# Three modulation vectors of a diffusion layer: elementwise sums on three engines, or products on TensorE

## The chip, the cores and the metric

The kernel runs on one core of a Trainium2 chip. The core has a matrix engine (TensorE, PE in the profile, with PEld for its weight loads), three engines for elementwise work (VectorE or DVE, ScalarE or ACT, GpSimd or POOL) and a queue on SyncE (SP) that issues all of this kernel's transfers. Each engine works through its own instructions in order and waits for others through semaphores. The metric is the device time of one execution in microseconds (us); lower is better.

## The reference, cut to what matters

Two layers act on 1024 latent tokens and 256 context tokens of width 1024. Every layer is modulated by six vectors per sample, once for the latent tokens and once for the context:

```python
silu_c = jax.nn.silu(c)
silu_cc = jax.nn.silu(c_ctx)
for l in range(DEPTH):
    mod = (silu_c @ w_mod[l] + b_mod[l])[:, None, :]
    mod_c = (silu_cc @ w_mod[l] + b_mod[l])[None, None, :]
    sh_m, sc_m, gt_m, sh_f, sc_f, gt_f = jnp.split(mod, 6, axis=-1)
    ...
    h = modulate(x, g_pre_mix[l], sh_m, sc_m)          # vectors 0 and 1
    y, yc = mixer(h, hc, ...)                          # attention and pooling
    x = x + gt_m * rmsnorm(y, g_post_mix[l])           # vector 2
    h = modulate(x, g_pre_ffn[l], sh_f, sc_f)          # vectors 3 and 4
    x = x + gt_f * rmsnorm(swiglu(h, ...), g_post_ffn[l])   # vector 5
```

The weights `w_mod[l]` are 1024 x 6144 in float32, so one vector reads 1024 x 1024 numbers, 4 MB, and multiplies them by only two columns (the activations of `c` and `c_ctx`). Layer 0 has dense attention (8 heads over all 1280 keys) beside a pooling mixer, layer 1 windowed attention; both end in a gated feed-forward part.

## The kernel before, in words

Activations lie feature-major: 128 features on the partitions, tokens along the row. Precision is kept by splitting a float32 operand into a rounded part and a rest (names ending in h and l: `wh`, `wl`, `hh`, `hl`, `ph`, `pl`) and adding three products. The latent tokens go in two chunks of 512 (L0, L1), the context in one of 256 (CC).

**Order.** The program is not written in the order in which it runs. `Plan` records every operation with what it depends on, `merge` interleaves parts of the record by giving each a stretch of positions, and `layout` then places all operations on the five engines by a list scheduling with a table of costs: an engine takes, of what is ready, the operation with the lowest position. Tiles come from shared pools, 38 large buffers of 4 KB a partition (tag `Q`, names beginning with `Q_`), 19 small ones of 2 KB (tag `S`), 8 banks of PSUM (`ps`). A tile that lies more than a given number of positions ahead must leave a reserve free (`AHEAD_OF`). Loads are allowed up to 30 us of PE work ahead (`LOAD_WINDOW`); a transfer is put down as 1100 ns to its start, its bytes over 360 per ns (4 bytes an element), and 1500 ns to its landing. Everything is issued from one line, so that the profile puts L419 on every instruction; the groups are told apart by their tiles.

**The stage around the change.** Vectors 0 and 1 of layer 0 are needed first. `mod_row` computes them at the start of the kernel on PE: the two columns of `c2` are the stationary operand, a 128 x 512 piece of weights (tile `S_wm`) streams past, eight such products add up in one PSUM bank, and the two rows that result (`S_row`) are turned into columns by four small transposes. Vectors 2, 3 and 4 (`MODLATE`) come later. After the first projections, one stage merges three streams: attention of L0 and CC (`attend0`); the pooling mixer with the projections of L1 (`poolmix`, `proj0`); and `mod_vec` for vectors 2, 3 and 4, followed by `fin_post` and `fin_pre`, which combine them with gains. The merge gives attention the first nine tenths of the stretch (`SHARES[0]`) and the others all of it. Then come the output projection of L0 and CC and the residual with its norms (`rest`, `chain`), which read these vectors first.

**The elementwise form.** `mod_vec` takes a vector in two halves of 512 outputs and loads eight pieces of 128 x 512 (tag `MW`, three buffers, tile `mw`). For each of the two columns it keeps an accumulator `S_ma` of 128 x 512. Of the eight pieces, with `POOLC = 2`, four go to DVE (one multiply or multiply-add each) and four are scaled on ACT (into `S_mp`, the first into the accumulator itself) and added on POOL. At the end PE transposes the accumulator in four blocks, DVE sums along the row (`mc`) and adds the bias. `mod_vec` also computes vector 5 of layer 0 and all of layer 1, in other stages.

Of the kernel before, what the change touches and what calls it, by code (L numbers as in the profile page):

```python
# [10 lines left out]
F32 = mybir.dt.float32  # L11
F32R = mybir.dt.float32r
AF = mybir.ActivationFunctionType
ALU = mybir.AluOpType
# [4 lines left out]
P = 128  # L19
D = 1024  # L20
KT = D // P
# [30 lines left out]
POOLC = 2  # L52
# [16 lines left out]
class Plan:  # L69
# [73 lines left out]
    def add(self, eng, op, args, kw):  # L143
# [29 lines left out]
        for n in tiles:  # L173
            self.tiles[n][3] += 1
        cost, fset = self.cost(eng.name, op, args, kw, outs, ins)
        load = eng.name == "SP" and all(a.space == DRAM for a in ins)
        if eng.name == "DVE":
            port = op != "stream_shuffle" and all(a.space != PSUM for a in ins + outs)
        else:
            port = eng.name == "PL" and op != "memset"  # L180
        self.ops.append((eng, op, args, kw, deps, tiles, cost, fset, i + self.bias, load, self.phase, port))

    def cost(self, e, op, args, kw, outs, ins):
        o = outs[0] if "out" in kw or e != "ACT" else args[0]
        if op == "dma_start":
            n = 4 * self.free(o) * list(o.ap)[0][1]
            return max(56.0, n / 360.0), None
        if e == "PE":
            mv = args[2]
            n = self.free(mv)  # L190
            if op == "transpose":
                return max(54.0, n / 1.2) + 2.7, None
            return max(104.0, n / 2.4 + 13.0) if mv.dtype == F32R else max(216.0, n / 0.6) + 2.7, None
        n = max(self.free(a) for a in ins + [o]) if ins else self.free(o)
        ps = any(a.space == PSUM for a in ins)
        ptr = any(self.free(a) == 1 for a in ins) and n > 1
        if e == "ACT":
            c = (51.0 if ins[0].space == PSUM else 93.0) + n / 1.2
            c += 93.0 * (self.is_ap(kw.get("bias")) or self.is_ap(kw.get("scale"))) + 93.0 * ("accum_out" in kw)
            return c, self.SETS.get(args[2].name)  # L200
        if e == "PL":
            return {"tensor_tensor": 160 + 2.13 * n, "tensor_scalar": 175 + 3.34 * n}.get(op, 40), None
        if op == "reciprocal":
            return 69 + 6.25 * n, None
        if op in ("tensor_copy", "tensor_scalar", "memset"):
            return 69 + 61 * ptr + n * (1.0417 if ps else 0.5208), None
        if op == "tensor_tensor_reduce":
            return 129 + 1.0417 * n, None
        return 69 + 61 * (ptr and op == "scalar_tensor_tensor") + 1.0417 * n, None
# [29 lines left out]
    def layout(self):  # L239
# [58 lines left out]
        while len(order) < n:  # L298
# [38 lines left out]
            for q in set(early) - {e}:  # L337
                for _, j in avail[q]:
                    heapq.heappush(future[q], (ready[j], ops[j][8], j))
                avail[q].clear()  # L340
            eng, op, args, kw, deps, tiles, cost, fset, pr, load, _, port = ops[i]
            moved = set()
            for tl in tiles:
# [83 lines left out]
def tile_dit(  # L427
# [4 lines left out]
    plan = Plan(tc.nc)  # L432
    T, S, V, G, SP = plan.engines
# [7 lines left out]
    def nm(s):  # L441
        uid[0] += 1
        return f"{s}{uid[0]}"

    def qt_(shape, dt, s="q"):
        return sb.tile(shape, dt, tag="Q", name=nm("Q_" + s), bufs=NQ)

    def st(shape, dt, s="s"):
        return sb.tile(shape, dt, tag="S", name=nm("S_" + s), bufs=NS)

    def small(shape, dt, s="t"):
        return sb.tile(shape, dt, tag="T", name=nm(s), bufs=24)

    def pst(n=512, dt=F32):
        t = ps_p.tile([P, 512], dt, tag="ps", name=nm("ps"), bufs=8)
        return t[:, :n]
# [37 lines left out]
    ident = cst.tile([P, P], F32, name="ident")  # L494
# [6 lines left out]
    c2 = cst.tile([P, KT, 2], F32, name="c2")  # L501
    bm = cst.tile([P, 2, 6, KT], F32, name="bm")
# [4 lines left out]
    mod = cst.tile([P, 2, 6, 2, KT], F32, name="mod")  # L507
# [131 lines left out]
    def mod_row(l, v0, nv):  # L639

        for b in range(2):
            acc = [pst() for _ in range(nv)]
            for k in range(KT):
                for v in range(nv):
                    w = st([P, 512], F32, "wm")
                    o = (v0 + v) * D + b * 512
                    SP.dma_start(out=w, in_=w_mod[l, k * P:(k + 1) * P, o:o + 512])
                    T.matmul(acc[v][0:2, :], c2[:, k, :], w, start=(k == 0), stop=(k == KT - 1))
            tp = pst()
            for v in range(nv):  # L650
                row = st([P, 512], F32, "row")
                S.activation(row[0:2, :], acc[v][0:2, :], AF.Copy)
                for j in range(4):
                    i = v * 4 + j
                    T.transpose(tp[:, 2 * i:2 * i + 2], row[0:2, j * P:(j + 1) * P], ident[0:2, 0:2])
            tv = tp[:, 0:nv * 8].rearrange("p (v k c) -> p v c k", v=nv, c=2)
            for v in range(nv):
                for c in range(2):
                    V.tensor_tensor(mod[:, l, v0 + v, c, b * 4:b * 4 + 4], tv[:, v, c, :], bm[:, l, v0 + v, b * 4:b * 4 + 4], op=ALU.add)

    def mod_vec(l, v, cs, pool=0):


        for half in range(2):
            acc = [st([P, 512], F32, "ma") for _ in cs]
            for k in range(KT):
                w = sb.tile([P, 512], F32, tag="MW", name=nm("mw"), bufs=3)
                o = v * D + half * 512
                SP.dma_start(out=w, in_=w_mod[l, k * P:(k + 1) * P, o:o + 512])
                for a, c in zip(acc, cs):  # L670
                    if (k + 2 * c) % 4 < pool:
                        t = a if k == 0 else st([P, 512], F32, "mp")
                        S.activation(t, w, AF.Copy, scale=c2[:, k, c:c + 1])
                        if k:
                            G.tensor_tensor(a, a, t, op=ALU.add)
                    elif k == 0:
                        V.tensor_scalar(a, w, c2[:, k, c:c + 1], None, op0=ALU.mult)
                    else:
                        V.scalar_tensor_tensor(a, w, c2[:, k, c:c + 1], a, op0=ALU.mult, op1=ALU.add)
            for a, c in zip(acc, cs):  # L680
                tp = pst()
                for j in range(4):
                    T.transpose(tp[:, j * P:(j + 1) * P], a[:, j * P:(j + 1) * P], ident)
                col = small([P, 4], F32, "mc")
                V.reduce_sum(col, tp.rearrange("p (j i) -> p j i", j=4), axis=AX.X)
                V.tensor_tensor(mod[:, l, v, c, half * 4:half * 4 + 4], col, bm[:, l, v, half * 4:half * 4 + 4], op=ALU.add)
# [5 lines left out]
    def fin_post(l, kind, cs=(0, 1)):  # L692
        for c in cs:
            V.tensor_tensor(fin[:, l, 2 * kind + 1, c, :], mod[:, l, 3 * kind + 2, c, :], gn[:, 2 * kind + 1, l, :], op=ALU.mult)
# [511 lines left out]
    plan.bias = 0  # L1206
    a = len(plan.ops)
    mod_row(0, 0, 2)
    fin_pre(0, 0)
    b = len(plan.ops)  # L1210
# [62 lines left out]
    a = len(plan.ops)  # L1273
# [18 lines left out]
    a = len(plan.ops)  # L1292
# [5 lines left out]
    b = len(plan.ops)  # L1298
# [8 lines left out]
    h = None  # L1307
    c = len(plan.ops)
    for v in MODLATE:
        mod_vec(0, v, (0, 1), POOLC)  # L1310
    fin_post(0, 0)
    fin_pre(0, 1)
    plan.merge(a, b, c, share=SHARES[0])
# [18 lines left out]
    a = len(plan.ops)  # L1332
# [4 lines left out]
    b = len(plan.ops)  # L1337
# [8 lines left out]
    a = len(plan.ops)  # L1346
    ws = ffn_pair(0, tt, SIZES[0][0], hc)
# [3 lines left out]
    b = len(plan.ops)  # L1351
# [9 lines left out]
    a = len(plan.ops)  # L1361
# [45 lines left out]
    b = len(plan.ops)  # L1407
# [22 lines left out]
    a = len(plan.ops)  # L1430
    mix = newmix(half(L0, 1))
    attend1(L0, 1, mix, AHEADS[3])
    b = len(plan.ops)
# [9 lines left out]
    a = len(plan.ops)  # L1443
# [3 lines left out]
    b = len(plan.ops)  # L1447
# [9 lines left out]
    ws = ffn_pair(1, tt, SIZES[2][0])  # L1457
# [102 lines left out]
```

## Time and profile before

| what | value |
|---|---|
| median of 3 runs | 2748.66 us (2748.55 to 2752.36) |
| the profiled execution's own time | 2747.63 us |
| its span, first to last instruction | 2745.8 us |
| granted TensorE clock, mean | 0.983 |
| busy: PE, DVE, ACT, POOL | 96%, 73%, 50%, 12% |
| moved by DMA | 481.06 MB, 175 GB/s on the mean |
| loads of modulation weights `mw` | 160 of 256 KB, 48 of them for the three vectors (130 to 361 us) |

A group's row reads: line, engine, operation, the tile written and the tiles read, their shape, the count; then busy us and the mean ns of one; then the engine's idle time just before these instructions and what ended it. A row of stages by window gives the length first and then busy us with a count for each engine. Busy time of PE is the union of its instructions' times, whose ends overlap the next one's start; two PE instructions that follow each other are therefore spaced closer than the duration of one.

### The profile page before, as it was taken

The numbers are of one execution on the slowest core, as the hardware profiler recorded it, in microseconds if no ns is written. First come the engines' busy times: TensorE is split into PE (matmuls) and PEld (weight loads), VectorE is DVE, ScalarE is ACT, GpSimd is POOL, SyncE is SP. The second block draws the span as 40 slices with busy tenths as digits, with TensorE's granted clock in tenths as the row PEclk, the third lists the DMA queues.
The fourth block names the chain that finished last, engine by engine and source line by source line (L and its number), as shares of the span: only waits on it lengthen the run. The fifth ranks groups of instructions, "written<-read, shape, count | busy, mean of one in ns | idle before, by whom it ended". The sixth has DMA issues, their size and how long they took to land.

```text
span 2745.8 us, 39261 instructions
## 1 busy us (share of the span) xinstructions
PE 2637.9 (96%) x13781; PEld 2186.7 (80%) x13781; DVE 1996.6 (73%) x3684; ACT 1361.9 (50%) x2846; POOL 319.5 (12%) x277
## 2 busy tenths in 40 slices
PE   8989898999999999999999999998999999999997
PEld 4766677888888888888878878787878788888887
DVE  4779887866559998866484688898882798872335
ACT  4468875666554333331143467677784534332011
POOL 0353532000020000000011400330000300000001
PEclk9999999999999999999999999998999999999999
DMA  7334457333566666686543635353335545556252
GB/s 285 114 102 147 141 200 276 121 110 122 177 200 216 219 215 222 226 320 223 206 151 113 219 101 190 103 176 120 116 101 203 192 173 203 196 183 253 112 184 77
DMA packets 240902, 481.06 MB, mean 175 GB/s; under 512 B 24128, under 2 KB 85824, under 8 KB 240704
## 3 DMA queue, kind: packets, MB, share of 16 engines
q1 hardware_dynamic: 240704, 478.54, 50.7%
q8 instruction: 109, 1.79, 0.3%
q14 instruction: 89, 0.73, 0.1%
HBM read 350.52 MB, written 123.99 MB: 173 GB/s over the span
## 4 chain that ended last, share of the span: by engine, by line
PE 71%; DVE 11%; ACT 4%; DMA 3%; issue 2%; POOL 1%; SPq 0%; DVEq 0%; ACTq 0%; POOLq 0%
PE ps L419 71%; DVE Q_x L419 1%; DVE S_fw L419 1%; DVE ps L419 1%; DVE mx L419 1%; ACT S_ph L419 1%; DVE Q_hl L419 1%; ACT Q_p L419 1%; DVE Q_yf L419 1%; DVE S_sq L419 1%; DMA Q_raw<-in_wo_in 1%; DVE Q_tl L419 1%; ACT S_p L419 1%; DVE S_pl L419 1%; DVE Q_wl L419 1%
## 5 line engine op out<-in xcount | busy, mean ns | idle before, releaser
L419 PE MATMUL ps<-Q_ac,Q_wh 128*128 128x512 f32 (+1 forms) x1920 | 530.3, 358 | 0.8 <-ACT Q_wh L419 0.5
L419 PEld LDWEIGHTS ps<-Q_ac,Q_wh 128*128 128x128 f32 x1920 | 343.2, 191 | 50.1 <-DVE Q_yf L419 0.6
L419 PE MATMUL ps<-Q_hh,Q_wh 128*128 128x512 f32 (+1 forms) x992 | 365.2, 377 | 6.8 <-ACT Q_hh L419 3.5
L419 PE MATMUL ps<-Q_hl,Q_wh 128*128 128x512 f32 (+1 forms) x992 | 362.6, 374 | 1.9 <-DVE Q_hl L419 1.8
L419 ACT ACTIVATE Q_wh<-Q_raw 128x1024 fp32r<-128x1024 f32 x202 | 212.4, 1063 | 303.9 <-PE ps L419 134.8
L419 PE MATMUL ps<-Q_ac,Q_wl 128*128 128x512 f32 (+1 forms) x960 | 341.7, 357 | 3.3 <-DVE Q_wl L419 3.3
L419 DVE TENSOR_TENSOR Q_wl<-Q_raw,Q_wh 128x1024 fp32r<-128x1024 f32 x190 | 235.3, 1248 | 137.7 <-ACT Q_wh L419 112.7
L419 PE MATMUL ps<-Q_tl,Q_wh 128*128 128x512 f32 x704 | 275.8, 392 | 3.1 <-DVE Q_tl L419 3.1
L419 PE MATMUL ps<-Q_th,Q_wh 128*128 128x512 f32 x704 | 275.5, 392 | 1.2 <-ACT Q_th L419 1.2
L419 PE MATMUL ps<-Q_kt,S_q 128*128 128x256 f32 (+3 forms) x992 | 255.0, 340 | 18.5 <-DVE Q_x L419 7.2
L419 PE MATMUL ps<-Q_hh,Q_wl 128*128 128x512 f32 (+1 forms) x992 | 265.9, 373 | 0.0
L419 DVE TENSOR_TENSOR S_pl<-ps,S_ph 128x512 fp32r<-128x512 f32 (+1 forms) x328 | 213.1, 672 | 69.2 <-ACT S_ph L419 64.7
L419 DVE TENSOR_TENSOR Q_yf<-Q_yf,ps 128x512 f32<-128x512 f32 (+1 forms) x200 | 116.9, 589 | 200.1 <-PE ps L419 199.7
L419 ACT ACTIVATE S_ph<-ps 128x512 fp32r<-128x512 f32 (+1 forms) x328 | 186.0, 604 | 88.3 <-PE ps L419 84.8
L419 PEld LDWEIGHTS ps<-Q_hh,Q_wh 128*128 128x128 f32 x992 | 189.8, 192 | 38.7 <-ACT Q_hh L419 5.1
L419 PEld LDWEIGHTS ps<-Q_hl,Q_wh 128*128 128x128 f32 x992 | 190.1, 192 | 30.2 <-DVE Q_hl L419 3.4
L419 PEld LDWEIGHTS ps<-Q_kt,S_q 128*128 128x128 f32 x992 | 171.0, 195 | 47.5 <-issue 12.6
L419 PEld LDWEIGHTS ps<-Q_ac,Q_wl 128*128 128x128 f32 x960 | 182.7, 190 | 28.3 <-DVE Q_wl L419 4.0
L419 PEld LDWEIGHTS ps<-Q_hh,Q_wl 128*128 128x128 f32 x992 | 175.8, 191 | 27.2
L419 PE MATMUL ps<-ident,Q_p 128*128 128x128 f32 x928 | 185.3, 277 | 10.6 <-DVE S_pl L419 3.1
L419 ACT ACTIVATE Q_p<-ps,nb 128x256 f32<-128x256 f32 (+1 forms) x336 | 185.3, 562 | 15.1 <-DVE nb L419 14.7
L419 PE MATMUL ps<-Q_th,Q_wl 128*128 128x512 f32 x704 | 188.8, 390 | 0.0
(194 smaller groups left out, 5208.9 us busy)
## 6 DMA issues: line engine op xcount, KB each, us to landing
Q_raw<-in_w_ffn_in SPq DMA_DIRECT2D x132, 512.0 KB, 4.7
a_scr_l<-S_act SPq DMA_DIRECT2D x176, 256.0 KB, 2.1
Q_ac<-a_scr_l SPq DMA_DIRECT2D x88, 512.0 KB, 6.1
mw<-in_w_mod SPq DMA_DIRECT2D x160, 256.0 KB, 3.5
Q_raw<-in_w_ffn_out SPq DMA_DIRECT2D x66, 512.0 KB, 6.8
S_q<-q_scr_l SPq DMA_DIRECT2D x192, 128.0 KB, 3.7
g_scr<-S_gs SPq DMA_DIRECT2D x88, 256.0 KB, 2.0
Q_gs<-g_scr SPq DMA_DIRECT2D x44, 512.0 KB, 5.5
```

Source lines behind the costliest of these rows:

```text
L419: getattr(eng.real, op)(*args, **kw)
```

## The change

A new function `mod_mm` takes the place of `mod_vec` for vectors 2, 3 and 4 of layer 0. It computes a half of a vector as `mod_row` does, with c2 as the stationary operand and both columns in one product. It differs from `mod_row` in its loads: a half's weights come in four transfers of 512 KB into four large buffers (`Q_wm`), and `plan.gate` makes all eight products depend on the last of the four loads. ACT copies the two rows out of PSUM, four small transposes turn them, and DVE adds the bias. `mod_vec` stays for the other vectors. `mod_mm` uses no accumulator in SBUF, no `MW` buffer and nothing on POOL.

The second edit is to the planner's table: a product with a float32 moving operand of n columns is put down as n/1.2 ns, at least 104, in place of n/0.6 ns, at least 216. That covers the products of `mod_mm`, those of `mod_row`, the sums with `ones2` in `rstd` and the sums of squares with `selg`. Prices decide only the order in which instructions are issued.

```diff
-            return max(104.0, n / 2.4 + 13.0) if mv.dtype == F32R else max(216.0, n / 0.6) + 2.7, None
+            return max(104.0, n / 2.4 + 13.0) if mv.dtype == F32R else max(104.0, n / 1.2) + 2.7, None
...
+    def mod_mm(l, v):
+
+        for b in range(2):
+            ws = []
+            for k in range(0, KT, 2):
+                w = qt_([P, 2, 512], F32, "wm")
+                o = v * D + b * 512
+                SP.dma_start(out=w, in_=w_mod[l, k * P:(k + 2) * P, o:o + 512].rearrange("(a p) n -> p a n", p=P))
+                ws += [w[:, 0, :], w[:, 1, :]]
+            plan.gate = len(plan.ops) - 1
+            acc = pst()
+            for k, w in enumerate(ws):
+                T.matmul(acc[0:2, :], c2[:, k, :], w, start=(k == 0), stop=(k == KT - 1))
+            plan.gate = None
+            row = st([P, 512], F32, "row")
+            S.activation(row[0:2, :], acc[0:2, :], AF.Copy)
+            tp = pst()
+            for j in range(4):
+                T.transpose(tp[:, 2 * j:2 * j + 2], row[0:2, j * P:(j + 1) * P], ident[0:2, 0:2])
+            tv = tp[:, 0:8].rearrange("p (k c) -> p c k", c=2)
+            for c in range(2):
+                V.tensor_tensor(mod[:, l, v, c, b * 4:b * 4 + 4], tv[:, c, :], bm[:, l, v, b * 4:b * 4 + 4], op=ALU.add)
...
     for v in MODLATE:
-        mod_vec(0, v, (0, 1), POOLC)
+        mod_mm(0, v)
     fin_post(0, 0)
     fin_pre(0, 1)
```

## The prediction

> **What bounds the kernel now.** I read the page first, then busy time by stage, then the groups of the stage that the change touches.
>
> ```profile
> span 2745.8 us, 39261 instructions
> PE 2637.9 (96%) x13781; PEld 2186.7 (80%) x13781; DVE 1996.6 (73%) x3684; ACT 1361.9 (50%) x2846; POOL 319.5 (12%) x277
> PE   8989898999999999999999999998999999999997
> ```
>
> TensorE (PE) is busy 96% of the span, so an edit that adds PE work looks bad at once. That share is a mean over unlike stages, though. The stages by window (length; then busy us and count for PE, its weight load, DVE, ACT, POOL; granted clock; DMA share; GB/s):
>
> ```profile
> 130.00:390.00 260.00, 233.56 (x1202) 174.54 (x1200) 227.00 (x409) 202.16 (x473) 116.55 (x129) 0.99 0.48 157
> 390.00:450.00 60.00, 58.95 (x318) 50.94 (x316) 42.63 (x56) 30.34 (x50) 21.80 (x16) 1.00 0.70 244
> 600.00:800.00 200.00, 199.80 (x1104) 170.29 (x1104) 108.75 (x186) 109.16 (x230) 21.77 (x12) 1.00 0.44 151
> 1600.00:2060.00 460.00, 431.54 (x2634) 368.09 (x2633) 399.43 (x1073) 348.05 (x947) 50.58 (x40) 0.96 0.40 126
> ```
>
> All the edited work lies in 130 to 390 us: attention of the first half of the latent tokens merged with the second half's projections, the pooling mixer and the three modulation vectors. There PE is not full. VectorE (DVE) is busy 227.0 of 260 (87%) and ScalarE (ACT) 202.2 (78%). In the other attention stage in which PE has gaps, 1600 to 2060, DVE stands at 399.4 of 460, again 87%; where DVE is at 54% (600 to 800) or 71% (390 to 450), PE is busy all but 0.1% and 2% of the time. So I read 87% as about what DVE reaches in this chain of hand-overs, and DVE with ACT, not PE, as the bound of this stage.
>
> PE's busy time overstates its load, since matmul ends overlap. So I count what PE needs. Its largest groups in 130 to 390:
>
> ```profile
> L419 PE MATMUL ps<-ident,Q_p 128*128 128x128 f32 x352 | 64.0, 276 | 6.3 <-DVE S_pl L419 2.8 <-ACT Q_p L419 1.9 <-DVE mc L419 0.5
> L419 PE MATMUL ps<-Q_kt,S_q 128*128 128x512 f32 x128 | 45.3, 433 | 3.9 <-ACT Q_p L419 2.9 <-DVE nb L419 0.6 <-DVE S_pl L419 0.5
> L419 PE MATMUL ps<-S_pl,Q_vt 128*128 128x512 f32 x88 | 38.2, 435 | 1.4 <-DVE S_pl L419 1.4
> L419 PE MATMUL ps<-S_ph,Q_vt 128*128 128x512 f32 x88 | 38.2, 434 | 6.4 <-ACT S_ph L419 4.9 <-DVE S_pl L419 1.4
> L419 PE MATMUL ps<-Q_hl,Q_wh 128*128 128x512 f32 x92 | 37.3, 413 | 0.0
> L419 PE MATMUL ps<-Q_hh,Q_wh 128*128 128x512 f32 x90 | 37.1, 418 | 0.4 <-ACT Q_wh L419 0.4
> L419 PE MATMUL ps<-Q_hh,Q_wl 128*128 128x512 f32 x96 | 29.9, 406 | 0.0
> L419 PE MATMUL ps<-Q_kt,S_q 128*128 128x256 f32 x96 | 20.7, 308 | 0.5 <-ACT Q_p L419 0.3
> L419 PE MATMUL ps<-ident,S_ma 128*128 128x128 f32 x48 | 9.7, 275 | 0.3 <-DVE S_fw L419 0.2
> ```
>
> What one costs when the next follows at once, from runs in the timeline (start, length, count), and from the start of the kernel, which already computes two modulation vectors by the very product that the change adds:
>
> ```profile
> 1201.41 1.07 PE L419 MATMUL ps<-Q_th,Q_wl 128*128 128x512 f32 x4
> ...
> 1202.77 0.39 PE L419 MATMUL ps<-Q_ac,Q_wl 128*128 128x512 f32 x1
> ```
> ```profile
> 372.43 1.03 PE L419 MATMUL ps<-ident,Q_p 128*128 128x128 f32 x8
> ```
> ```profile
> 23.11 0.40 PE L419 MATMUL ps<-ident,S_row 2*128 2x2 f32 x4
> ...
> 24.86 10.46 PE L419 MATMUL ps<-S_wm,c 128*2 128x512 f32 x24
> ```
> ```profile
> L419 PE MATMUL ps<-S_wm,c x64: 591/592/1062, 4.1 to 42.1; 128*2 128x512 f32 x64
> ```
>
> A split-precision product of 512 columns: (1.07 - 0.39) / 3 = 0.227 us; one of 256 columns I take at half, 0.114. A transpose: (1.03 - 0.276) / 7 = 0.108. The full-precision product of a weight half: (10.46 - 0.592) / 23 = 0.429. Need of the stage: 582 x 0.227 + 96 x 0.114 + 400 x 0.108 = 132.1 + 10.9 + 43.2; the other 124 of the 1202 instructions are small groups of mixed width, at a mean of 0.165 another 20.5. Together 206.7 us of 260: PE has 53 us to spare here.
>
> **The change, part by part.** DVE, ACT and POOL, with the rows of 130 to 390 that go:
>
> ```profile
> L419 DVE SCALAR_TENSOR_TENSOR S_ma<-mw,c,S_ma 128x512 f32<-128x512 f32 x42 | 38.1, 916 | 0.8 <-POOL S_ma L419 0.7
> ...
> L419 DVE TENSOR_REDUCE mc<-ps 128x4 f32<-128x512 f32 x10 | 6.8, 682 | 0.7 <-PE ps L419 0.6
> ...
> L419 DVE TENSOR_SCALAR S_ma<-mw,c 128x512 f32<-128x512 f32 x6 | 3.8, 640 | 0.0
> L419 DVE TENSOR_TENSOR mod<-mc,bm 128x4 f32<-128x4 f32 x10 | 3.4, 337 | 0.0
> ```
> ```profile
> L419 ACT ACTIVATE S_mp<-mw,c 128x512 f32<-128x512 f32 x42 | 29.7, 731 | 1.9 <-POOL S_ma L419 1.7
> ...
> L419 ACT ACTIVATE S_ma<-mw,c 128x512 f32<-128x512 f32 x6 | 4.4, 731 | 8.2 <-DMA mw<-in_w_mod 8.2
> ```
> ```profile
> L419 POOL TENSOR_TENSOR S_ma<-S_ma,S_mp 128x512 f32<-128x512 f32 x42 | 55.3, 1318 | 64.3 <-ACT S_mp L419 32.6 <-DVE S_ma L419 28.7 <-DVE rz L419 1.3
> ```
>
> What comes in has its rows at the start of the kernel:
>
> ```profile
> L419 ACT ACTIVATE S_row<-ps x4: 569/586/587, 22.4 to 43.1; 2x512 f32<-2x512 f32 x4
> ```
> ```profile
> L419 DVE TENSOR_TENSOR mod<-ps,bm x8: 149/152/163, 24.6 to 44.4; 128x4 f32<-128x4 f32 x8
> ```
>
> DVE loses 38.1 + 6.8 + 3.8 + 3.4 = 52.1 and gains 10 x 0.152 = 1.5: 227.0 becomes 176.4. ACT loses 29.7 + 4.4 = 34.1 and gains 6 x 0.586 = 3.5: 202.2 becomes 171.6. POOL loses 55.3 of 116.6.
>
> PE loses 48 transposes (48 x 0.108 = 5.2) and gains 48 products (48 x 0.429 = 20.6) and 24 tiny transposes (six times 0.40 = 2.4): net +17.8, to 224.5.
>
> The Trainium skill's page "FP8 and Floating Point Precision", section "TensorE Precision Notes", says that true FP32 takes four passes through the array. By that rule one product would be an estimated 4 x 0.227 = 0.91 us and the 48 together 43.6, so that PE would need 247.5. This kernel's row disagrees: 0.429 is 1.9 times 0.227, and the measurement decides.
>
> If DVE could be filled to the same 87%, the stage would need 176.4 / 0.87 = 203 us; ACT by the same share 197; PE at a complete fill 224.5. So PE becomes the bound of the stage and the length follows from how full it gets. Bounds: as full as now, 206.7 / 260 = 79.5%, gives 282 us, a loss of 22; quite full, as in 600 to 800, with 3% lost to hand-overs gives 231 us, a gain of 29. At some 242 us DVE is at 73% and ACT at 71%. The nearest row is 390 to 450 with DVE at 71%, where PE was busy 98%; ACT was lighter there (51%), and the stage still begins and ends in chains, so I take 93%: 224.5 / 0.93 = 241.4, a **gain of 18.6**.
>
> Loads. 48 loads of 256 KB become 24 of 512 KB, the same bytes, in the pool of 38 large buffers instead of three own ones. All loads go through SP's queue in program order, and these are its long waits from 130 to 450 (us, times, longest):
>
> ```profile
> SPq L419 <- DVE S_ma L419: 73.3, 26, 8.8
> SPq L419 <- POOL S_mo L419: 44.6, 11, 7.3
> SPq L419 <- ACT S_mo L419: 35.1, 9, 10.5
> ```
> ```profile
> Q_raw<-in_we_in SPq DMA_DIRECT2D x8, 512.0 KB, 5.2
> ```
>
> The first wait (a buffer that an elementwise sum still reads) goes; SP waits instead for PE to release a large buffer. The other two stay: a store waits for its producer and every load behind it waits too. The change also adds a wait: the planner sets a half's eight products behind the last of its four loads, at a landing that it puts 1.1 + 1.46 + 1.5 = 4.06 us after issue; a load of this size takes 5.2 here. If PE reaches the group just then, it stands 1.1 us, and behind it everything in its queue: scores, transposes, value products, and so DVE and ACT. Six groups, 6.8 us at most from this alone; at the least nothing, since loads may run up to 30 us of PE work ahead. I take 2, nearer to nothing because of that lead.
>
> New price in the planner. It halves the price of wide full-precision products (0.856 to 0.429), which now meets the measured 0.429. At the start this may put the 64 products' loads earlier or later among others. The bounds are PE's idle time there: it waited 6.0 us for those weights
>
> ```profile
> L419 PE MATMUL ps<-S_wm,c 128*2 128x512 f32 x64 | 32.3, 652 | 6.2 <-DMA S_wm<-in_w_mod 6.0
> ```
>
> so at best 6 us are won, and as much may be lost by the same waits doubled. I take 0. Later stages are ordered anew by the same planner; PE is full in most of them, and I take 0 there too, within the same 6 us.
>
> A result that comes late costs nothing at first: the old sums end at 396 us, and their first reader (the residual scale) starts at 444.6, which leaves 48 us of cover.
>
> ```profile
> L419 DVE TENSOR_TENSOR mod<-mc,bm x12: 86/155/1089, 203.5 to 396.5; 128x4 f32<-128x4 f32 x12
> ```
> ```profile
> 444.56 1.41 DVE L419 SCALAR_TENSOR_TENSOR Q_y<-Q_y,fin,ps 128x512 f32<-128x512 f32 x2 [0.80 <-PE ps L419]
> ```
>
> **Sum:** -18.6 + 2 + 0 = -16.6 us. The profiled execution took 2747.6 (span 2745.8 and 1.8 around it), 1.0 below the median 2748.7. So 2748.7 - 16.6 = **2732 us**. From 390 us on PE is full, so what is won before moves the rest forward without being eaten by it.
>
> **Rivals.** (A) *PE fills up.* With DVE and ACT down to three quarters, PE runs as in 600 to 800: 231 us, a gain of 29, 2748.7 - 29 = 2720. For it: the two rows with DVE at 54% and 71%. Against: this stage has many short hand-overs per product.
>
> (B) *The relief only pays the bill.* PE's gaps come from latency (transpose, split on ACT, subtraction on DVE, product), not from engine load. It then gets just the products into its gaps: 2749, no change. For it: PE's idle before its groups is a few us each, spread over many releasers. Against: 53 us of room and the same 87% twice.
>
> (C) *Late weights, slower.* A group of products reaches the head of PE's queue while its fourth load is held in SP's queue behind a store. The price is the mean wait of the row on POOL, 44.6 / 11 = 4.1 us, plus the 1.1 us of the landing: 6 x 5.2 = 31. With 31 for my 2: 2732 + 29 = 2761. It decides from 18.6 us in all, 3.1 per group; from there on nothing is left of the gain. For it: 80 us of such waits in the stage. Against: loads go ahead of need, and POOL, one cause of those waits, loses half its work.
>
> (D) *PE's additions lie on the chain and nothing is relieved:* 2748.7 + 17.8 = 2766. Against it speaks the DVE row. (E) *The four passes are real here:* 247.5 / 0.93 = 266 us of stage, 2748.7 + 6 + 2 = 2757; the x24 row all but excludes it. (F) *The change doesn't do what it says:* the planner puts the groups so late that the residual waits; over the 48 us of cover only, and then about 2749.
>
> **How the numbers follow.** My forecast 0.57 (its own range 2722 to 2743); A 0.15; B 0.12; C 0.09; D 0.04; E 0.01; F 0.02. This kernel's times can be told from no change at about 0.2%, 5.5 us: faster means below 2743.2, slower above 2754.2. Faster: 0.57 + 0.15 = 0.72, and 0.02 of B's spread: 0.74. Slower: C, D, E: 0.14. Same: 0.12. The range runs from 2714 (A with the start's 6 us) to 2753 (B with a few us of late loads): it leaves out C and D and a little besides, some 0.17.
>
> **What would show it.** The stage that now ends near 390 should end near 373, with DVE and ACT at about 73% and 71% of it and PE's count of work at 224 us; the 48 products should take 0.43 us apart and follow each other without waits for their loads; PE's idle before groups released by DVE and ACT should shrink by more than half. From there to the end, all stages should be as long as they were. I am wrong if PE's idle time in the stage stays near 26 us (B, D), if PE shows waits of over 3 us for the modulation weights (C), or if the gain or loss lies in stages after 450 us, which would be the planner's new order and not the engines' load.

## The result, and the profile after

The changed kernel takes 2788.27 us (median; 2786.43 to 2789.38) against 2748.61 us before: a ratio of 1.0144, with a 95% interval of 1.0128 to 1.0160. It is 39.7 us **slower**; the forecast was 2732 us, faster.

The page of the changed kernel begins:

```profile
span 2786.6 us, 39164 instructions
PE 2686.7 (96%) x13853; PEld 2190.0 (79%) x13853; DVE 1954.4 (70%) x3624; ACT 1341.0 (48%) x2804; POOL 258.6 (9%) x235
PE   8999999899999999999999998998999999999997
```

DVE, ACT and POOL lost 42, 21 and 61 us of busy time over the whole span (51, 31 and 55 were forecast). PE gained 48.8 us of busy time and 72 instructions, where the prediction had 48 products and 24 tiny transposes for 48 transposes: 24 instructions more. The 48 that are too many are the heart of this case. Stages of the kernel before, cut at marks that both kernels have (last store of L0's queries; last result of attention on L0; first residual scale, of L0; that of the context; that of L1; first residual scale behind a feed-forward part):

```profile
0.00:128.00 128.00, 116.62 (x533) 73.98 (x534) 74.46 (x130) 62.21 (x116) 18.68 (x19) 0.99 0.55 192
128.00:369.00 241.00, 214.69 (x1110) 162.59 (x1110) 210.77 (x379) 185.62 (x441) 113.08 (x126) 0.99 0.47 151
369.00:445.00 76.00, 74.83 (x375) 59.52 (x375) 55.85 (x80) 43.51 (x77) 23.76 (x18) 1.00 0.67 227
445.00:486.00 41.00, 31.47 (x192) 27.51 (x191) 38.60 (x66) 29.26 (x58) 5.00 (x3) 0.83 0.57 214
486.00:795.00 309.00, 307.12 (x1715) 261.21 (x1714) 188.65 (x342) 178.92 (x393) 23.72 (x16) 0.99 0.40 137
795.00:1395.00 600.00, 598.80 (x3228) 517.32 (x3227) 478.55 (x766) 204.45 (x324) 4.93 (x3) 1.00 0.66 229
1395.00:2746.00 1351.00, 1294.37 (x6639) 1084.54 (x6637) 949.68 (x1926) 657.89 (x1439) 130.35 (x93) 0.98 0.46 158
```

The same stages of the changed kernel:

```profile
0.00:136.00 136.00, 118.99 (x513) 73.86 (x514) 78.36 (x134) 63.20 (x118) 23.19 (x23) 0.95 0.52 183
136.00:393.00 257.00, 248.39 (x1189) 163.77 (x1188) 164.98 (x321) 160.13 (x397) 54.21 (x81) 1.00 0.42 132
393.00:478.00 85.00, 83.08 (x386) 59.58 (x387) 51.83 (x73) 43.62 (x77) 21.01 (x16) 1.00 0.67 230
478.00:520.00 42.00, 31.86 (x191) 27.80 (x190) 38.78 (x66) 29.36 (x58) 4.94 (x3) 0.80 0.56 205
520.00:829.00 309.00, 306.39 (x1712) 260.73 (x1711) 188.23 (x341) 179.26 (x393) 23.24 (x16) 0.99 0.40 136
829.00:1430.00 601.00, 599.46 (x3229) 517.19 (x3228) 478.17 (x766) 206.76 (x325) 4.94 (x3) 1.00 0.65 229
1430.00:2787.00 1357.00, 1298.48 (x6643) 1087.12 (x6641) 954.09 (x1926) 658.62 (x1439) 127.06 (x93) 0.97 0.46 158
```

By length: +8 before the edited stage, +16 in attention, +9 in the part that finishes it, then +1, 0, +1, and +6 in everything after 1395 us. DVE falls from 87% to 64% of the attention stage and ACT from 77% to 62%, so the relief did arrive, while PE rises from 89% to 97%: the bound has moved to PE. The view of the new weight tiles says why:

```profile
L419 PE MATMUL ps<-Q_wm,c x96: 591/592/593, 175.5 to 421.0; 128*2 128x512 f32 x96
L419 SPq DMA_DIRECT2D Q_wm<-in_w_mod x24: 367/407/985, 153.7 to 366.4; - x24
```

24 transfers bring 48 pieces of 128 x 512, and PE executes **96** instructions on them. A float32 product is two TensorE instructions. The row that the prediction quoted from the start of the kernel said so already: 64 instructions, and the loads beside it are of 32 pieces:

```profile
L419 SPq DMA_DIRECT2D S_wm<-in_w_mod x32: 327/328/925, 1.2 to 34.0; - x32
```

### The profile page after: what moved, and what is told of

The parts are those of the page before. It is cut to its first block, busy times and chain, and to the rows that moved or that the text cites. A ratio compares the mean times of both kernels' runs of the same rounds, so it can differ in the third digit from the quotient of the medians.

```text
span 2786.6 us, 39164 instructions
## 1 busy us (share of the span) xinstructions
PE 2686.7 (96%) x13853; PEld 2190.0 (79%) x13853; DVE 1954.4 (70%) x3624; ACT 1341.0 (48%) x2804; POOL 258.6 (9%) x235
## 3 DMA queue, kind: packets, MB, share of 16 engines
q1 hardware_dynamic: 240320, 478.54, 49.6%
## 4 chain that ended last, share of the span: by engine, by line
PE 69%; DVE 8%; ACT 3%; DMA 2%; issue 1%; SPq 0%; POOL 0%; DVEq 0%; ACTq 0%
PE ps L419 69%; DVE Q_x L419 1%; DVE ps L419 1%; DVE S_fw L419 1%; DVE mx L419 1%; DVE Q_tl L419 1%; DVE Q_yf L419 1%; DVE Q_hl L419 1%; ACT S_p L419 1%; DVE S_sq L419 0%; ACT Q_p L419 0%; DVE S_pl L419 0%; DVE Q_wl L419 0%; DVE S_t L419 0%; ACT S_ph L419 0%
```

## The experiments

Each variant was timed beside the kernel before on the same chip. Ratios are to that kernel, with 95% intervals.

**The new price alone.** The kernel before with the planner's second edit and nothing else:

```diff
-            return max(104.0, n / 2.4 + 13.0) if mv.dtype == F32R else max(216.0, n / 0.6) + 2.7, None
+            return max(104.0, n / 2.4 + 13.0) if mv.dtype == F32R else max(104.0, n / 1.2) + 2.7, None
```

> The kernel before with only the planner's new price (n/1.2 for a float32 product); the three vectors stay elementwise sums. Theory 1 (the products themselves are the cost: the trace after holds 96 TensorE instructions for 48 products, 0.429 us each, 41 us, and some 12 us more for changing between kinds of products 41 times): price alone costs little, 2745 to 2762, most of it the 8 us by which the stage before 136 us is already later. Theory 2 (the price misleads the planner, and its order costs the time): most of the 40 us are here, 2770 to 2790.

Measured: 2759.91 against 2748.45 us, ratio 1.0050 (1.0031 to 1.0069): 11.5 us. That is within the first theory's range and far from the second's. The price is under a third of the loss, not its body.

**The products under the old price.** The changed kernel with that line put back:

```diff
-            return max(104.0, n / 2.4 + 13.0) if mv.dtype == F32R else max(104.0, n / 1.2) + 2.7, None
+            return max(104.0, n / 2.4 + 13.0) if mv.dtype == F32R else max(216.0, n / 0.6) + 2.7, None
```

> The changed kernel with the old price (n/0.6 = 853 ns for a product of 512 columns, which is what two instructions of 0.429 us take). Theory 1: still slow by the products' PE time, 2770 to 2785, some 10 us better than the changed kernel since the plan now knows what they cost. Theory 2: 2745 or less.

Measured: 2775.85 against 2748.45, ratio 1.0112 (1.0088 to 1.0136): the products alone cost 27.4 us. With the price's 11.5 that makes 38.9 of the 39.7: the two edits add up.

**No vectors at all.** Vectors 2, 3 and 4 of layer 0 are their biases alone; their weights are neither read nor multiplied, so this time is that of a kernel with part of the computation left out. The 12 MB of loads go with the sums.

```diff
     for v in MODLATE:
-        mod_vec(0, v, (0, 1), POOLC)
+        for c_ in range(2):
+            V.tensor_scalar(mod[:, 0, v, c_, :], bm[:, 0, v, :], 1.0, None, op0=ALU.mult)
```

> The kernel before without the work on the three vectors: vectors 2, 3 and 4 of layer 0 are their biases alone, with no weights read, no sums and no products. It measures what taking the sums away is worth by itself. If VectorE and ScalarE bound the stage, as the prediction has it, the stage of 260 us shrinks to some 217 (201.5 us of PE work at 93%): 2700 to 2712. If the gaps of PE come from latency, the stage gets shorter by little more than the 5 us of removed transposes: 2735 to 2745.

Measured: 2726.22 against 2748.45, ratio 0.9924 (0.9906 to 0.9943): the elementwise sums, with their loads, cost 22.2 us. Both expectations missed: the relief is real, but half of what the prediction's reading of the bound implied. From the last store of L0's queries to the first residual scale the run without vectors shows

```profile
131.00:348.00 217.00, 203.13 (x1061) 156.69 (x1060) 165.61 (x313) 157.82 (x394) 56.92 (x84) 0.98 0.33 108
348.00:424.00 76.00, 74.37 (x374) 59.40 (x373) 51.46 (x68) 42.75 (x75) 21.76 (x16) 1.00 0.69 238
```

Attention takes 217 us in place of 241, with DVE at 76%, ACT at 73% and PE still busy only 94%: PE waits for results (its longest wait in total, from 130 to 390 us, is 6.0 us for `Q_p` of ACT) even when no other engine is near its limit. Which of the things left out, work of DVE, of ACT, of POOL or the loads, bought the 22.2 us is not told apart. Against this kernel without vectors, the products under the old price cost 2775.85 - 2726.22 = **49.6 us**, against 22.2 for the sums.

**One unbroken run for each half.** The old price, and the planner sees a half's eight products as one operation, at eight times their price and 300 ns:

```diff
-            for k, w in enumerate(ws):
-                T.matmul(acc[0:2, :], c2[:, k, :], w, start=(k == 0), stop=(k == KT - 1))
+            T.block(acc[0:2, :], c2, *ws)
...
+            if op == "block":
+                for k in range(KT):
+                    eng.real.matmul(args[0], args[1][:, k, :], args[2 + k], start=(k == 0), stop=(k == KT - 1))
+                continue
```

> The changed kernel with the old price and each half's eight products kept as one unbroken run on TensorE (6 runs in place of 41). Theory 1: the changes between kinds of products fall from 41 to 6, worth 35 x 0.30 = 10 us of PE work: some 10 us under the run with the old price, 2760 to 2775. If these changes are hidden or cost nothing, the same time as with the old price, or some us more, because a block of 6.9 us holds up attention's scores behind it.

Measured: 2772.08, ratio 1.0090 (1.0073 to 1.0107), 3.8 us under the run with the old price, with intervals that overlap: less than the 10 expected. From 130 us to the first residual scale the run with the old price, and then this one, show

```profile
130.00:472.70 342.70, 331.89 (x1560) 221.89 (x1559) 219.71 (x397) 206.95 (x476) 76.56 (x100) 1.00 0.49 159
130.00:466.90 336.90, 322.00 (x1542) 223.40 (x1541) 219.94 (x395) 204.18 (x473) 76.55 (x100) 0.99 0.49 159
```

PE's busy time fell by 9.9 us (an estimated 4 of it belong to the 18 instructions fewer, at the mean of 0.21 us), but its idle time rose from 10.8 to 14.9: part of what the unbroken runs save comes back as waiting. This run's timeline shows best what one half costs:

```profile
172.63 7.03 PE L423 MATMUL ps<-Q_wm,c 128*2 128x512 f32 x16
```

Eight products are 16 instructions and 7.03 us: (7.03 - 0.592) / 15 = 0.429 each, 0.858 for a product. Six halves are 41.2 us.

**The products twice.** The old price, with the eight products repeated (the second set starts the sum anew):

```diff
-            for k, w in enumerate(ws):
-                T.matmul(acc[0:2, :], c2[:, k, :], w, start=(k == 0), stop=(k == KT - 1))
+            for j in range(2):
+                for k, w in enumerate(ws):
+                    T.matmul(acc[0:2, :], c2[:, k, :], w, start=(k == 0), stop=(k == KT - 1))
```

> The run with the old price, but each half's eight float32 products are made twice (the second set starts the sum anew, so the result is the same): 96 more TensorE instructions, 41.2 us, nothing else. If TensorE is the bound of the stage once the sums are gone, nearly all of it shows: 2776 + 35 to 50 = 2811 to 2826. If the stage still waits mostly for other engines and the products fall into gaps of TensorE, 2780 to 2800.

Measured: 2821.04, ratio 1.0265 (1.0247 to 1.0284), 45.2 us over the run with one set. Its weight-tile view has

```profile
L419 PE MATMUL ps<-Q_wm,c x192: 590/592/593, 166.5 to 458.9; 128*2 128x512 f32 x192
```

96 instructions more cost 45.2 us, 0.47 each, and they need 0.429: once the sums are gone, all of PE's extra work shows in the time. The second set has no loads, no gate and no transposes of its own. The first set, with all of these, cost 49.6, so that by this comparison they are worth some 4 us together.

**Products in the rounded type.** The columns c2 are split into a rounded part and a rest (four stationary columns), ACT rounds the weights, and the part of the weights below the rounding is left out, which is a part of the computation. The gate goes, and the price is the old one.

```diff
+                wh = qt_([P, 2, 512], F32R, "mh")
+                S.activation(wh, w, AF.Copy)
+                ws += [wh[:, 0, :], wh[:, 1, :]]
...
-                T.matmul(acc[0:2, :], c2[:, k, :], w, start=(k == 0), stop=(k == KT - 1))
+                T.matmul(acc[0:4, :], c4[:, k, :], w, start=(k == 0), stop=(k == KT - 1))
```

> The three vectors as products in the rounded type (fp32r) in place of float32, old price: ScalarE rounds the weights, the columns are split into rounded part and rest (4 stationary columns), the rest of the weights (their part below the rounding) is left out. If the cost of the change is that a float32 product is two TensorE instructions of 0.429 us and changes the kind of product around it, then 48 instructions at 0.227 us stand here (10.9 us in place of 41) and the time falls to that of the kernel without the vectors plus about 13 us of TensorE work and up to 10 for ScalarE: 2736 to 2750. If the cost comes from the loads in large buffers, the held PSUM bank or the order of the plan, it stays at 2765 to 2780.

Measured: 2742.22 against 2749.66, ratio 0.9969 (0.9953 to 0.9984): **faster than both kernels**. Its tile view:

```profile
L419 PE MATMUL ps<-Q_mh,c x48: 387/397/479, 158.3 to 381.1; 128*4 128x512 f32 x48
...
L419 ACT ACTIVATE Q_mh<-Q_wm x24: 1041/1060/1107, 157.2 to 344.3; 128x1024 fp32r<-128x1024 f32 x24
```

The loads and their buffers are the same (24 more large tiles hold the rounded weights); now 48 instructions for 48 products, of the kind that follows at 0.227 us. The loss is gone, 33.6 us under the run with float32 products, although ACT does 25 us more. So the loads and buffers were not the cause. The gate went too in this run, but the changed kernel's view of these tiles lists no wait for their loads, and the doubled products, which add nothing to the gate, cost their full time.

**The rounding on GpSimd.** The same, with the planner's price for it added:

```diff
-                S.activation(wh, w, AF.Copy)
+                G.tensor_copy(wh, w)
```

> The rounded run (rest of the weights left out) with the 24 roundings on GpSimd in place of ScalarE. ScalarE loses 25 us of work in the stage. If the rounded run is bound by TensorE's need alone, the same time, 2738 to 2746. If ScalarE's roundings still hold up attention's splits and exponentials, up to 8 us less: 2731 to 2738. If GpSimd's slower copies make the products late, above 2746.

Measured: 2741.66 against 2747.56, ratio 0.9981 (0.9969 to 0.9993). That is the rounded run's time within the intervals: ACT's 25 us lay beside other work, as the first case has it.

**The rest of the weights too.** GpSimd subtracts the rounded weights from the weights, and eight more products a half add them, so that nothing is left out:

```diff
+                wl = qt_([P, 2, 512], F32R, "ml")
+                G.tensor_tensor(wl, w, r32(wh), op=ALU.subtract)
+                ls += [wl[:, 0, :], wl[:, 1, :]]
...
+                T.matmul(acc[0:4, :], c4[:, k, :], ls[k], start=False, stop=(k == KT - 1))
```

> As the rounded run, with the rest of the weights too: GpSimd subtracts the rounded weights from the weights, and 16 products of 0.227 us a half add up (96 instructions, 21.8 us), which is as precise as the other products of this kernel. By TensorE's work alone 11 us above the rounded run: 2747 to 2762; over that if GpSimd's 24 subtractions of some 2.6 us hold up the pooling mixer.

Measured: 2763.96 against 2749.66, ratio 1.0042 (1.0028 to 1.0056); 21.7 us over the rounded run, where 11 were expected from TensorE alone. The subtractions take 2.4 us each on POOL, beside the work of attention and the pooling mixer:

```profile
L419 POOL TENSOR_TENSOR Q_ml<-Q_wm,Q_mh 128x1024 fp32r<-128x1024 f32 x24 | 57.4, 2403 | 35.7 <-ACT Q_mh L419 21.4 <-PE ps L419 13.8 <-ACT Q_wh L419 0.4
```

From 130 us to the first residual scale PE is busy 14 us longer than in the rounded run and idle 7 us longer. It waited for the subtractions directly only 1.1 us in this profile; its longest waits are for ACT (4.7 us for `S_ph`, 4.1 for `Q_p`). That POOL makes the other 11 us is argued, not shown.

**One vector by products.** Old price; vector 4 by `mod_mm`, vectors 2 and 3 by `mod_vec`:

```diff
-        mod_mm(0, v)
+        if v == 4:
+            mod_mm(0, v)
+        else:
+            mod_vec(0, v, (0, 1), POOLC)
```

> Vector 4 by float32 products, vectors 2 and 3 by elementwise sums, old price. All three by products cost 27 us, all three left out win 22. If both sides are linear in the number of vectors, one by products costs a third, 9 us: 2755 to 2760. If the relief of VectorE and ScalarE is worth most for the first vector taken away (half of the 22 or more against 16 for the products): 2750 to 2755 or less.

Measured: 2765.69 against 2749.66, ratio 1.0047 (1.0033 to 1.0060): 16.0 us, beyond both expectations. A third of the products' 49.6 is 16.5, so taking one vector's sums away bought next to nothing here. The trace shows where. From the last store of L0's queries to the last result of attention, and from there to the first residual scale:

```profile
131.00:375.00 244.00, 217.56 (x1094) 163.67 (x1093) 202.44 (x362) 176.84 (x425) 98.71 (x113) 0.97 0.41 133
375.00:466.00 91.00, 91.00 (x403) 60.67 (x403) 52.21 (x78) 45.16 (x79) 20.24 (x16) 1.00 0.67 240
```

All 32 instructions of vector 4 start from 378.7 us on, in the part that finishes attention, where PE was full already (74.8 of 76 us before); that part is 15 us longer than before. Attention itself takes 244 us against 241, though a third of the sums is gone. Why that third buys nothing there stays open.

**Wide products' price alone.** The kernel before, with the new price only for more than two columns:

```diff
-            ... else max(216.0, n / 0.6) + 2.7, None
+            ... else max(104.0 if n > 2 else 216.0, n / 1.2) + 2.7, None
```

> The kernel before with the new price for wide float32 products alone (512 or 256 columns: the two early vectors and the sums of squares of the heads); the 2-column sums of the norms keep the old price. The new price for all cost 11 us. The wide ones take 0.858 us by the trace (two instructions of 0.429), so their new price is half the truth: if that misleads the plan, the 11 us are here, 2756 to 2762. If the narrow ones do it: 2746 to 2751.

Measured: 2755.48 against 2749.66, ratio 1.0020 (1.0008 to 1.0033): half of the price's cost, a little under the range that put all of it here. The last store of L0's queries is issued at 134.3 us, 6.0 behind the kernel before (128.3); with the whole new price it is 7.1 behind (135.4). The wide price, half the truth, goes with the late start; the rest belongs to the narrow one or to the new order as a whole.

**A price 3% lower, and 3% higher.** The kernel before with n/0.62, and in another run with n/0.58:

```diff
-            ... else max(216.0, n / 0.6) + 2.7, None
+            ... else max(216.0, n / 0.62) + 2.7, None
```

> The kernel before with the price of a float32 product 3% lower (n/0.62 in place of n/0.6), no other edit: how much the time moves when the planner only orders a little differently. If the order's own scatter is small, 2745 to 2754 and the 5 to 11 us of the runs with the new price are that price's doing. If it is 5 us and more to either side, those runs can't be told from scatter.

> As the run before it, with the price 3% higher (n/0.58). The same two outcomes: 2745 to 2754, or 5 us and more to either side.

Measured: 2748.46 and 2748.45 against 2747.56, ratios 1.0005 (0.9995 to 1.0015) and 1.0003 (0.9993 to 1.0012): no change. These small steps reorder little, though: a comparison of PE's 13781 instructions in order, line by line, with those of the kernel before gives 16 and 46 lines of difference, against 92 for the wide price and 884 for the whole one. So they show that the order doesn't scatter the time by itself at that size; they don't bound what a reordering as large as the whole price's may do.

## Why the prediction was wrong

**The step that failed: "48 products (48 x 0.429 = 20.6)".** The duration was right, the count was not. 0.429 us is the spacing of instructions, and every float32 product is two of them: 96 x 0.429 = 41.2. PE's additions were 38.4 us net in place of 17.8. The x96, the x16 in 7.03 us, the doubled run's 45.2 us and the rounded run's 48 instructions all show it. The number stood in the prediction's own quoted row, x64; dividing by the 32 pieces that the code multiplies there would have found it. The Trainium skill's page "FP8 and Floating Point Precision", section "TensorE Precision Notes", says that true FP32 takes four passes through the array. The trace agrees: a product takes 0.858 us, against the estimate of 4 x 0.227 = 0.91 worked out from that rule; how four passes fall on two instructions, no run shows. The prediction compared one instruction with the rule for a product and turned the rule down. Rival E, which had this cost, got a chance of 0.01; its time, 2757 us, is still 31 below the measured one, since it too took 93% for PE's fill and nothing for the price.

**PE's fill, "93%".** Too high. From the window of 260 us the prediction's method gives 201.5 / 0.93 = 217 us without the vectors, a gain of 43; measured were 22.2. The reading that PE did not bound this stage was right in kind: the run without vectors gained 22 us where PE lost 5 us of work; but with DVE at 76% of attention PE was still idle, and 390 to 450 us, the stage taken as the model, is mostly projections with few hand-overs. Idle time is also the smaller part of what the fill lacks. In the 217 us of attention without vectors PE idles 14 us, and at the prediction's own prices its instructions need an estimated 182; the other 20 us are wider spacing. Products of 512 columns that follow each other there with no idle time recorded between them start 0.257 us apart on the mean (384 pairs), where the prediction priced them by an unbroken run at 0.227. What widens the spacing is not shown. With the right count and the fill that this run implies, 201.5 / (260 - 22.2) = 85%, worked out afterwards, the stage would have been forecast at (224.5 + 20.6) / 0.847 = 289 us, 29 over the 260; under the old price 27.4 were measured.

**The price, "I take 0", bounds of 6 us.** It cost 11.5. The prediction called the new price right because 0.429 "meets the measured 0.429"; it is half of what a product takes. The bound came from one wait at the start and was too narrow. With the new price alone, 7.1 of these 11.5 us are there by the last store of L0's queries.

**Late loads, "I take 2", and rival C.** In the changed kernel from 130 to 424 us PE's longest waits in total are these, and none is for a modulation weight:

```profile
PE ps L419 <- ACT Q_p L419: 4.7, 8, 1.6
PE ps L419 <- DMA Q_kt<-S_kk: 1.2, 1, 1.2
PE ps L419 <- DVE S_pl L419: 1.2, 4, 0.6
```

PE never waited there for a weight of these vectors, though SP's waits behind stores did grow (on POOL's results from 44.6 to 92.2 us from the stage's start to the residual's norms):

```profile
SPq L419 <- POOL S_mo L419: 92.2, 12, 17.5
```

The slower side was forecast with the wrong mechanism: C is refuted. What happened is nearest to D (PE's additions on the path), with the additions doubled, but a relief of 22 us stands against them, where D had none. **The relief of DVE, ACT and POOL** came. In busy time it is a fifth less than forecast on DVE and a third less on ACT, yet no less work left than was forecast: the durations of all their instructions, added up, fell by 55.5 and 34.2 us. Busy time is the union of instructions that overlap their neighbours, and those overlaps shrank by 13 us on each. **The test that the prediction named**, PE's idle time in the stage, misled: the idle time fell as it said (to 8.6 us of 257), because the instructions that were not counted filled it.

## What to carry to other kernels

Divide the instructions in a row by the products in the code before pricing a product; the spacing of instructions is its price only if the count agrees. An engine that gets relief buys less than its busy share suggests where many short hand-overs link the engines: leaving the work out altogether, at first, tells about the most that a replacement can win (22 us here), and one that puts 41 us on the engine next in line did not win it. A planner's price should be that of what is issued, all instructions of the operation together.

## What the runs showed of the hardware

A float32 product of 512 columns with two stationary columns is two TensorE instructions, 0.858 us, 3.8 times the 0.227 of one in the rounded type; a transpose of float32 is one (48 instructions for the 48 blocks of `S_ma` before). Where a float32 product stands between rounded ones, the spacing around it grows:

```profile
224.46 0.50 PE L419 MATMUL ps<-S_dh,Q_wp 128*128 128x512 f32 x1
224.89 1.02 PE L419 MATMUL ps<-Q_wm,c 128*2 128x512 f32 x2
225.84 0.50 PE L419 MATMUL ps<-S_dl,Q_wp 128*128 128x512 f32 x1
226.17 0.40 PE L419 MATMUL ps<-S_dh,Q_wp 128*128 128x512 f32 x1
```

From the rounded product to the pair 0.43 us, over the pair 0.95 in place of 0.858, and then 0.33 to the next, where 0.227 is usual between rounded products; so this pair on its own costs 0.4 us beyond its instructions. It is one passage: over the changed kernel's attention stage a rounded product of 512 columns is followed by a pair after 0.345 us on the mean of 22. Joining the pairs into six runs took 3.8 us from the kernel's time, which the intervals don't separate from nothing.
